# A 32-byte tile at the top of the right-hand SBUF stack, ahead of the pool that holds the parts of X, in a fp32 two-layer transformer kernel

## The chip, the core and the metric

The kernel runs on one core of one Trainium2 chip. The metric is the device time of one launch in microseconds (us); the time given for a kernel is the median of its runs. One more execution was profiled, and all rows of a profile in this document come from profiled executions.

## The reference, cut to what matters

The input is 512 tokens of width 1024 in fp32. Two layers follow each other, each with a gated feed-forward block, a mixer and a second feed-forward block; the last step is a norm.

```
for layer in range(2):
    x = x + 0.5 * swiglu(rmsnorm(x, g[0]), ffn_w_in[layer, 0], ffn_w_out[layer, 0])
    h = rmsnorm(x, g[1])
    x = x + (even_mixer(h, ...) if layer == 0 else odd_mixer(h, ...))
    x = x + 0.5 * swiglu(rmsnorm(x, g[2]), ffn_w_in[layer, 1], ffn_w_out[layer, 1])
return rmsnorm(x, final_norm_g)
```

`swiglu` multiplies by a 1024 x 5632 matrix, gates one half with the silu of the other, and multiplies by a 2816 x 1024 matrix. The even mixer joins gated linear attention with softmax attention that has a forget gate; the odd mixer selects keys with an indexer and attends in a latent space. The output must be as exact as fp32.

## The kernel before, in words

X lies transposed in SBUF: 8 tiles of 128 features by 512 tokens. Every product of two fp32 operands is made of three fp32r products: each operand is split into a high part, which is a rounded copy (ScalarE), and a low part, which is the rest (DVE); high x high, high x low and low x high are summed in PSUM. `mm3` (L207 to L209) issues the three matmuls for one weight block of 128 x 128 and one moving operand of up to 512 columns.

The stages run one after the other: ffn0, even, ffn1, ffn2, odd, ffn3, and the final norm.

*The ffn stages.* The first product of a feed-forward block is done by Winograd's form of Strassen's scheme, seven products p1 to p7 in place of eight, on halves of the tokens (256 columns each) and on halves of the contracted features. `combined` (L231 to L259) makes from X the seven combinations of its quarters (`B11`, `T1`, `B21`, `B22`, `T2`, `T4`, `T3`) and splits them into `th` (high) and `tl` (low): four tiles of each, `[128, 7, 256]` fp32r, which stay for the whole stage. `product` (from L358, the matmul is L366) streams one of the seven slices of 256 columns against 128-column weight blocks: 2 halves of the output x 4 pairs of feature tiles x 3 parts, so 24 matmuls for each of the seven products. The outer loop is over 11 pairs of output tiles; pair 0 of the first stage is done the plain way with 512 columns (96 matmuls of `mm3` on `th`, `tl`). After pairs 3, 7 and 11 the second product of the block runs over what has been gated so far: `down_mm` streams `hh`, `hl` (512 columns) against weights (L207 to L209). The weights come by DMA on SyncE's queue into `wraw`, `a22` and `a12`; DVE combines them (`side`, L132 to L153) and ScalarE and DVE split them (`cut`, L162 and L163) into `whi`, `wlo`, up to three products ahead.

*The mixer stages.* They begin with projections of X. `scaled` (L218) splits X into eight tiles `xgh` and eight `xgl`, `[128, 512]` fp32r. `proj_units` streams them, 512 columns, against weight blocks. `tok_units` (L596 to L608) makes token-major values instead: there slices of 128 columns of `xgh`, `xgl` are the stationary weights, and 256 columns of `whi`, `wlo` are streamed.

*Where the tiles lie.* The tile framework gives out addresses in SBUF (bytes in each partition) from two stacks. The left stack grows up from the bottom; X, `wraw`, `whi`, `wlo`, `hh`, `hl` and the mixers' scratch (`x`, `p`, `pts` and others) lie there. The right stack grows down from the top, and has one pool only, `xp`. `open_in` (L1293) releases and opens it anew for each stage; it holds `th`, `tl`, `te`, `to`, `a22`, `a12` and `ws` in the ffn stages, `xgh` and `xgl` in the mixers, and `fo` at the end. The top of the right stack is byte 229344, which is 32 past a multiple of 64, and every tile of `xp` has a size that is a multiple of 64. So every tile of `xp` begins 32 bytes past a multiple of 64: `th0` at 147424, `tl3` at 197600, `xgh0` at 196576, `xgl0` at 212960. On the left, `X` (16512), `wraw` (47552), `whi` (63936), `wlo` (76224), `hh` (88512), `hl` (108992) and the `x` tiles begin at multiples of 64; `ones`, `ident`, `causal`, `chunkmask` and `cols` (from 33120) begin 32 past one. The pool `xp` reuses the place of scratch tiles of earlier stages, and a tile waits for those whose bytes it takes (`reuse_waits="tile"`).

The order of TensorE's instructions is the program's, written by hand; the other engines' orders are planned by the framework.

```
self.xp = tc.alloc_tile_pool(name="xp", bufs=1, side="right", reuse_waits="tile")
self.TH = [self.xp.tile([128, 7, HT], F32R, name=f"th{j}") for j in range(KT // 2)]
for i, (w, x) in enumerate(((hi, xh), (hi, xl), (lo, xh))):
    mm(o, w[:, c], x, start=fresh and f == j == i == 0, stop=j == 3 and i == 2, skip_group_check=True)
```

Of the kernel before, what the change touches and what calls it, by code (L numbers as in the profile page):

```python
# [8 lines left out]
F32 = mybir.dt.float32  # L9
# [163 lines left out]
class Builder:  # L173
# [1090 lines left out]
    def build(self):  # L1264
        from contextlib import ExitStack
        with ExitStack() as ctx:
            nc, tc = self.nc, self.tc
            pool = lambda name, bufs, **kw: ctx.enter_context(tc.tile_pool(name=name, bufs=bufs, **kw))
# [19 lines left out]
            for t, n in ((self.chunkmask, "chunkmask"), (self.ident, "ident"), (self.causal, "causal"), (self.cols, "cols")):  # L1288
                nc.gpsimd.dma_start(t, self.i[n])

            self.xp = None

            def open_in(kind):  # L1293
# [173 lines left out]
```

## Time and profile before

| what | value |
|---|---|
| median of 3 runs | 1914.0 us |
| the 3 runs | 1907.32, 1914.0, 1915.86 us |
| the profiled execution | 1906.54 us |
| its span, first to last instruction | 1904.7 us |
| mean granted TensorE clock | 0.991 |
| instructions in the profile | 30516 |
| HBM read, written | 178.03 MB, 2.15 MB |

The profiled execution is 1.8 us longer than its span, and is the fastest of those shown. Engines are named PE (TensorE's matmuls), PEld (TensorE's weight loads), DVE, ACT (ScalarE), POOL and SP. A tile's buffer numbers are left out, so `th` stands for th0 to th3. The end of a matmul in the profile is modelled, while its start is recorded; neighbours overlap in the listing.

### The profile page before, as it was taken

The page shows a single profiled execution, that of the slowest core. Times are in us where ns is not written, and L with a number is a line of the kernel's source. Part 1 is how long each engine was busy: PE and PEld are TensorE (multiplying, and loading weights), DVE is VectorE, ACT ScalarE, POOL GpSimd, SP SyncE. Part 2 cuts the span into 40 slices and gives each one's busy share as a digit, 9 for nine tenths or more (in the row PEclk, how much of TensorE's full clock was granted, in tenths as well). Part 3 has the DMA queues.
Part 4 walks back from the last instruction along what each step waited for, and adds up shares of the span by engine and source line. Part 5 has one row for each costly group of instructions (what it writes and reads, how often), then busy time and mean ns, then how long its engine had stood idle before and what let it go on. Part 6 is the DMA issues. An engine that isn't in the chain of part 4 may idle for free.

```text
span 1904.7 us, 30516 instructions
## 1 busy us (share of the span) xinstructions
PE 1858.3 (98%) x12376; PEld 1665.6 (87%) x12376; DVE 1451.5 (76%) x1917; ACT 909.9 (48%) x1286; POOL 218.0 (11%) x211
## 2 busy tenths in 40 slices
PE   8999999999999999999999999999999999999997
PEld 7989899887877999989899998987777789899996
DVE  8979687457557979868897885964898599696774
ACT  6535345334465634525564452543538566353353
POOL 0000000100262000000200000011258320000001
PEclk9999999999999999999999999999999999999998
DMA  5333422223441233322423333234156222423322
GB/s 186 96 107 105 126 86 78 94 80 96 126 122 67 89 110 104 113 97 78 144 89 92 109 100 122 67 107 136 60 162 170 79 94 93 125 89 114 108 67 78
DMA packets 60653, 198.16 MB, mean 104 GB/s; under 512 B 7896, under 2 KB 8072, under 8 KB 57440
## 3 DMA queue, kind: packets, MB, share of 16 engines
q1 hardware_dynamic: 57856, 191.65, 32.2%
q10 hardware_dynamic: 2304, 4.20, 0.8%
q8 instruction: 97, 1.59, 0.3%
q0 software_dynamic: 352, 0.36, 0.1%
q14 instruction: 44, 0.36, 0.1%
HBM read 178.03 MB, written 2.15 MB: 95 GB/s over the span
## 4 chain that ended last, share of the span: by engine, by line
PE 84%; DVE 12%; ACT 2%; issue 1%; DMA 1%; SPq 0%; DVEq 0%; POOL 0%; ACTq 0%; POOLq 0%
PE ps L366 25%; PE pt L366 12%; PE s L209 6%; PE s L208 6%; PE s L207 6%; PE s L366 6%; PE ps L207 3%; PE ps L208 3%; PE ps L209 3%; PE s L730 2%; DVE tl L241 2%; DVE wlo L88 1%; PE o L764 1%; DVE acc L1217 1%; PE pt L749 1%; PE pt L207 1%
## 5 line engine op out<-in xcount | busy, mean ns | idle before, releaser
L366 PE MATMUL ps<-th,wlo 128*128 128x256 f32 x1376 | 384.8, 280 | 2.4 <-DVE wlo L163 2.3
L366 PE MATMUL ps<-th,whi 128*128 128x256 f32 x1376 | 385.2, 280 | 1.3 <-DVE ta L414 1.3
L366 PE MATMUL ps<-tl,whi 128*128 128x256 f32 x1376 | 384.5, 279 | 0.9 <-DVE tl L241 0.9
L84 ACT ACTIVATE whi<-wraw 128x1024 fp32r<-128x1024 f32 (+3 forms) x156 | 157.3, 1010 | 351.0 <-PE s L208 135.5
L366 PEld LDWEIGHTS ps<-th,wlo 128*128 128x128 f32 x1376 | 259.4, 188 | 3.2 <-DVE wlo L163 3.2
L366 PEld LDWEIGHTS ps<-th,whi 128*128 128x128 f32 x1376 | 259.2, 188 | 2.3 <-DVE ta L414 1.5
L366 PEld LDWEIGHTS ps<-tl,whi 128*128 128x128 f32 x1376 | 259.3, 188 | 1.7 <-DVE tl L241 1.1
L209 PE MATMUL s<-hh,wlo 128*128 128x512 f32 x528 | 205.9, 390 | 0.0
L208 PE MATMUL s<-hl,whi 128*128 128x512 f32 x528 | 205.6, 389 | 0.0
L207 PE MATMUL s<-hh,whi 128*128 128x512 f32 x528 | 205.6, 389 | 0.0
L162 ACT ACTIVATE whi<-a 128x1024 fp32r<-128x1024 f32 x131 | 139.0, 1061 | 137.8 <-issue 39.2
L88 DVE TENSOR_TENSOR wlo<-wraw,whi 128x1024 fp32r<-128x1024 f32 (+3 forms) x144 | 169.2, 1176 | 40.3 <-ACT whi L84 39.8
L279 POOL TENSOR_TENSOR ss<-ss,sq 128x512 f32<-128x512 f32 x41 | 65.4, 1596 | 1113.6 <-ACT sq L275 1113.4
L366 PE MATMUL pt<-th,whi 128*128 128x256 f32 x688 | 192.0, 279 | 0.0
L366 PE MATMUL pt<-tl,whi 128*128 128x256 f32 x688 | 191.9, 279 | 0.0
L366 PE MATMUL pt<-th,wlo 128*128 128x256 f32 x688 | 191.9, 279 | 0.0
L163 DVE TENSOR_TENSOR wlo<-a,whi 128x1024 fp32r<-128x1024 f32 x131 | 159.7, 1219 | 6.8 <-ACT whi L162 6.7
L162 ACT ACTIVATE whi<-wraw 128x1024 fp32r<-128x1024 f32 (+1 forms) x89 | 93.6, 1052 | 131.7 <-PE ps L366 51.5
L492 DVE SCALAR_TENSOR_TENSOR dn<-s,R 128x512 f32<-128x512 f32 x72 | 49.7, 690 | 122.3 <-PE s L209 122.3
L162 ACT ACTIVATE whi<-ws 128x1024 fp32r<-128x1024 f32 x86 | 90.7, 1055 | 84.0 <-PE ps L366 51.2
L366 PEld LDWEIGHTS pt<-tl,whi 128*128 128x128 f32 x688 | 129.3, 188 | 0.0
L366 PEld LDWEIGHTS pt<-th,wlo 128*128 128x128 f32 x688 | 129.3, 188 | 0.0
(323 smaller groups left out, 4338.4 us busy)
## 6 DMA issues: line engine op xcount, KB each, us to landing
a<-in_ffn_in_dram SPq DMA_DIRECT2D x88, 512.0 KB, 3.7
wraw<-in_ffn_in_dram SPq DMA_DIRECT2D x87, 512.0 KB, 4.7
wraw<-in_ffn_out_dram SPq DMA_DIRECT2D x64, 512.0 KB, 3.6
wraw<-in_ffn_out_dram SPq DMA_DIRECT2D x32, 384.0 KB, 3.1
x<-x SPq DMA_DIRECT2D x62, 128.0 KB, 2.3
wraw<-in_even_fox_dram SPq DMA_DIRECT2D x4, 1024.0 KB, 4.8
wraw<-in_even_out_dram SPq DMA_DIRECT2D x4, 1024.0 KB, 5.6
wraw<-in_odd_q_dram SPq DMA_DIRECT2D x8, 512.0 KB, 3.2
```

What stands on the lines that cost most here:

```text
L84: nc.scalar.activation(hi, x, AF.Copy)
L88: nc.vector.tensor_sub(lo, x, hi.bitcast(F32))
L162: b.nc.scalar.activation(o[0][:, s], x[:, s], AF.Copy)
L163: b.nc.vector.tensor_sub(o[1][:, s], x[:, s], o[0][:, s].bitcast(F32))
L207: mm(ps, w[0], x[0], start=first, stop=False)
L208: mm(ps, w[0], x[1], start=False, stop=False)
L209: mm(ps, w[1], x[0], start=False, stop=last)
L241: v.tensor_sub(l, src, h.bitcast(F32))
L279: nc.gpsimd.tensor_tensor(self.ss, self.ss, sq, op=OP.add)
L366: mm(o, w[:, c], x, start=fresh and f == j == i == 0, stop=j == 3 and i == 2, skip_group_check=True)
L492: nc.vector.scalar_tensor_tensor(t, bank, 0.5, R, op0=OP.mult, op1=OP.mult)
L730: nc.tensor.matmul(s[:, :n], q[hh][:, b * 128:b * 128 + 128], k[hh][:, :n], start=k is kh, stop=k is kl)
```

## The change

Before the pool `xp` is opened for the first time, one pool of one tile is opened on the same side. The tile has 8 fp32 in each partition, 32 bytes; nothing writes or reads it, and it stays until the end. All tiles of `xp` get addresses that are 32 lower, multiples of 64: `th0` 147392, `xgh0` 196544, and so on.

```diff
             for t, n in ((self.chunkmask, "chunkmask"), (self.ident, "ident"), (self.causal, "causal"), (self.cols, "cols")):
                 nc.gpsimd.dma_start(t, self.i[n])
 
+
+            pool("edge", 1, side="right").tile([128, 8], F32, name="edge")
             self.xp = None
 
             def open_in(kind):
```

## Rows read from the trace of the kernel before

**Rows 1.** Busy time, share of the span and instructions, whole span (page).

```profile
PE 1858.3 (98%) x12376; PEld 1665.6 (87%) x12376; DVE 1451.5 (76%) x1917; ACT 909.9 (48%) x1286; POOL 218.0 (11%) x211
```

**Rows 2.** The chain that ended last, by engine and by line (page).

```profile
PE 84%; DVE 12%; ACT 2%; issue 1%; DMA 1%; SPq 0%; DVEq 0%; POOL 0%; ACTq 0%; POOLq 0%
PE ps L366 25%; PE pt L366 12%; PE s L209 6%; PE s L208 6%; PE s L207 6%; PE s L366 6%; PE ps L207 3%; PE ps L208 3%; PE ps L209 3%; PE s L730 2%; DVE tl L241 2%; DVE wlo L88 1%; PE o L764 1%; DVE acc L1217 1%; PE pt L749 1%; PE pt L207 1%
```

**Rows 3.** PE's groups: names, shapes, count | busy us, mean ns | idle before.

```profile
L366 PE MATMUL ps<-th,whi 128*128 128x256 f32 x1376 | 385.2, 280 | 1.3 <-DVE ta L414 1.3
...
L207 PE MATMUL s<-hh,whi 128*128 128x512 f32 x528 | 205.6, 389 | 0.0
...
L207 PE MATMUL ps<-xgh,whi 128*128 128x512 f32 x208 | 84.2, 405 | 0.0
...
L207 PE MATMUL ps<-whi,xgh 128*128 128x256 f32 x128 | 37.6, 294 | 0.0
```

**Rows 4.** Windows: busy us (instructions) by engine, granted clock, DMA share, GB/s.

```profile
core 0: us, PE busy (x) PEld busy (x) DVE busy (x) ACT busy (x) POOL busy (x), PEclk, DMA share, GB/s
1067.20:1145.60 78.40, 78.40 (x673) 78.37 (x672) 71.05 (x70) 43.19 (x48) 0.00 (x0) 1.00 0.31 100
1145.70:1188.90 43.20, 43.20 (x192) 35.77 (x191) 22.90 (x27) 8.82 (x9) 0.00 (x0) 1.00 0.38 119
1382.80:1421.80 39.00, 39.00 (x169) 31.33 (x168) 38.24 (x93) 12.20 (x16) 19.70 (x13) 1.00 0.63 178
...
614.00:634.00 20.00, 19.00 (x156) 18.40 (x155) 19.83 (x26) 12.07 (x18) 3.86 (x2) 1.00 0.20 61
```

**Rows 5.** Timeline of PE, L366 run, then `hh` run: start, listed us, instruction.

```profile
1067.22 0.28 PE L366 MATMUL ps<-th,whi 128*128 128x256 f32 x1
...
1145.62 0.39 PE L207 MATMUL s<-hh,whi 128*128 128x512 f32 x1
...
1146.78 0.39 PE L209 MATMUL s<-hh,wlo 128*128 128x512 f32 x1
...
1188.94 0.39 PE L209 MATMUL s<-hh,wlo 128*128 128x512 f32 x1
```

**Rows 6.** Timeline of PE, odd mixer, first and last of 168 matmuls.

```profile
1382.70 0.40 PE L207 MATMUL ps<-xgh,whi 128*128 128x512 f32 x1
...
1421.67 0.40 PE L209 MATMUL ps<-xgh,wlo 128*128 128x512 f32 x1
```

**Rows 7.** Timeline of PE, token-major projection, two starts 24 matmuls apart.

```profile
388.09 0.28 PE L207 MATMUL ps<-whi,xgh 128*128 128x256 f32 x1
...
390.93 0.28 PE L207 MATMUL ps<-whi,xgh 128*128 128x256 f32 x1
```

**Rows 8.** Timeline of PE, odd mixer, a pair of score matmuls.

```profile
1328.70 0.40 PE L1227 MATMUL s<-x 128*128 128x256 f32 x2
1328.94 0.40 PE L207 MATMUL ps<-xgh,whi 128*128 128x512 f32 x1
```

**Rows 9.** Timeline of PE's weight loads, two in a row.

```profile
508.87 0.19 PEld L207 LDWEIGHTS ps<-xgh,whi 128*128 128x128 f32 x1
508.98 0.19 PEld L208 LDWEIGHTS ps<-xgl,whi 128*128 128x128 f32 x1
```

**Rows 10.** Groups of ACT, then of DVE, columns as in rows 3.

```profile
L162 ACT ACTIVATE whi<-a 128x1024 fp32r<-128x1024 f32 x131 | 139.0, 1061 | 137.8 <-issue 39.2 <-PE pt L366 39.0 <-PE s L208 29.6
...
L162 ACT ACTIVATE whi<-wraw 128x1024 fp32r<-128x1024 f32 x87 | 92.3, 1061 | 131.2 <-PE ps L366 51.5 <-PE s L366 46.5 <-PE s L208 27.2
L162 ACT ACTIVATE whi<-ws 128x1024 fp32r<-128x1024 f32 x86 | 90.7, 1055 | 84.0 <-PE ps L366 51.2 <-PE s L208 30.0 <-DVE ws L146 2.0
...
L163 DVE TENSOR_TENSOR wlo<-a,whi 128x1024 fp32r<-128x1024 f32 x131 | 159.7, 1219 | 6.8 <-ACT whi L162 6.7
...
L163 DVE TENSOR_TENSOR wlo<-wraw,whi 128x1024 fp32r<-128x1024 f32 x87 | 106.1, 1221 | 14.2 <-ACT whi L162 14.2
```

## The prediction, made before the changed kernel was built or run

> **What bounds the kernel now.** I read the page's busy shares first: PE works 98% of the span, DVE 76% [rows 1]. A high PE share alone says little, because the listed ends of matmuls are modelled, so the second view is the chain that ended last: 84% of it is PE, and 43% is the one line L366 (25, 12 and 6 by bank) [rows 2]. So the pace at which PE starts one matmul after another sets the time. The third view, the groups of PE's lines, cannot give that pace: it lists 280 ns for a 256-column matmul and 389 to 405 ns for a 512-column one [rows 3], and neighbours overlap. The fourth view can. The timeline gives starts, so a pace is the distance between two starts divided by the matmuls between them; the windows show that the stretches used are full and the granted clock is 1.00 there [rows 4].
>
> The paces differ with where the operands lie. In the program as it is, everything in the right-hand pool begins 32 bytes past a multiple of 64, and everything on the left that TensorE reads in these stretches begins at a multiple of 64; slices inside a tile step by 512 bytes or more and keep that.
> - 512 columns streamed from `hh`, `hl` (left), weights left: 42.16 us between starts 5 and 191 of a run, 186 steps, **226.7 ns** [rows 5].
> - 512 columns streamed from `xgh`, `xgl` (right), weights left: 38.97 us for 167 steps, **233.4 ns** [rows 6].
> - 256 columns from `th`, `tl` (right), weights left, L366: 78.40 us for the run's 672 matmuls (7 products of 24 for each of 4 pairs), **116.7 ns** [rows 5]. That is exactly half of 233.4, so this pace goes by streamed columns, with nothing fixed per matmul.
> - 256 columns from the left, weights from the right (token-major projections): 2.84 us for 24 steps, **118.3 ns** [rows 7].
>
> **The change, part by part.** No instruction is added, removed or moved; no queue sees another order. The tile holds no data. All right-hand tiles slide down by 32 bytes together. Their overlap with left tiles of earlier stages could bring or drop a wait, but left tiles begin and end at multiples of 64 in that region, so no right tile crosses an edge by moving from 32 past a multiple to the multiple. Cost of waits: 0.
>
> *(a) L366.* There are 1376 matmuls of each of three kinds into `ps` [rows 3], and by the code 3 x 688 into `pt` and 3 x 344 into `s`: 7224. The case that the trace does not show is a long run of 256 columns with both operands at multiples of 64. Bounds: half of the 512-column pace on the left, 113.35 ns, or the 118.3 ns of rows 7. Two aligned score matmuls of 256 columns (L1227) take 0.24 us, 120 ns each as rounded, near 117 at best [rows 8]; but they stand alone between right-hand matmuls. The first five aligned 512-column matmuls behind L366 are also slow, 1.16 us or 232 ns each, before the run settles at 226.7 [rows 5], so a pair cannot show a settled pace. I take 113.35 because the settled right-hand pace halves exactly from 512 to 256 columns, and because the weight load does not forbid it: where nothing else holds it, two loads start 0.11 us apart [rows 9], less than 113. Gain: 116.67 - 113.35 = 3.32 ns each. Not all count. The first 144 matmuls of three of the four ffn stages run while DVE is 99% busy (19.83 of 20 us) and PE waits for DVE-made parts [rows 4], and some 480 at the first stage's start do too, by the same reason; that leaves about 6300. 6300 x 3.32 = **20.9 us**. In steady stretches DVE is busy 71.05 of 78.40 us [rows 4]; shortened by 672 x 3.32 ns = 2.2 us that is 71.05 / 76.2 = 93%, so DVE still covers. Were that cover gone, DVE's own 71.05 us would be the floor.
>
> *(b) Mixer projections from `xgh`, `xgl`,* 512 columns: 208 of each of three kinds into `ps` [rows 3] and 32 of each into `s`, 720. They go from 233.4 to 226.7, 6.7 ns. The 168 of rows 6 lie where DVE is busy 38.24 of 39 us [rows 4] and gain nothing that lasts. 552 x 6.7 = **3.7 us**. The 96 matmuls of the first pair add 96 x 6.7 = **0.6 us**.
>
> *(c) Token-major projections,* 3 x 128 = 384 [rows 3]: from 118.3 to 113.35, 4.95 ns, **1.9 us**; lower bound 0.
>
> What rows 7 show is that the two reads affect each other: 118.3 ns is slower than the weight load by itself (0.11 us) and than L366's 116.7 with the streamed side misplaced. The Trainium skill, page "SBUF — State Buffer", section "Who interferes with whom", says otherwise: TensorE has two independent read ports and never waits on anyone. By it alignment would be worth nothing and the sum would be 0; the trace disagrees with it by the 6.7 ns between rows 5 and 6.
>
> *(d) The other engines.* ScalarE's copy of 1024 columns takes 1061 ns from right-hand `a`, 1061 from left-hand `wraw`, 1055 from right-hand `ws`; DVE's low part 1219 and 1221 from `a` and `wraw` [rows 10]. Right and left differ by 6 ns at most, on engines that are not the bound: 0, and 86 x 6 ns = 0.5 us either way if it counted. Loads into right-hand tiles keep their size and shape: 0.
>
> Sum: 20.9 + 3.7 + 0.6 + 1.9 = **27.1 us**. The profiled execution took 1906.5 us, so it would take 1879.4; the median shown is 1914.0, 7.5 above it, so I forecast 1914.0 - 27.1 = **1887 us**. What is late next is DVE at the start of each ffn stage, as now.
>
> **The rivals.**
> 1. *Only the 512-column matmuls gain.* With 256 columns the weight load fills nearly the whole step, and the two reads may keep each other at 35/32 of a cycle per column whatever the address, as the 117 ns or so of rows 8 suggest. Then (b) and the first pair alone count: 1914.0 - 4.3 = 1909.7. Against it: rows 8 are unsettled pairs.
> 2. *Half the gain.* The weight load, slowed by the stream beside it, holds the step at 115 ns: 6300 x 1.67 = 10.5, plus 4.3, plus (c) at half, 1.0: 1898. For it: rows 7, where some such slowing exists.
> 3. *The address does not matter,* or the tile does not move the pool. Then 226.7 against 233.4 comes from what runs beside (DVE 53% busy in the one stretch, 98% in the other [rows 4]): 1914. Against it: L366, with DVE at 91%, has the pace of the 98% stretch to the tenth of a ns, which a load on other engines would not give. This is also where the skill's rule named above leads.
> 4. *Slower.* Stream and weights now begin at the same place within 64 bytes and collide in every step without settling, as in the first five of rows 5: 232 / 226.7 = 1.023, so L366 goes to 119.4 ns. 7224 x 2.7 = 19.7 us lost, less 4.3: 1929. It decides against the change above 116.67 + 4.3 us / 7224 = 117.3 ns. Against it: aligned 512-column runs do settle, within five matmuls.
>
> **How the numbers follow.** About 0.5% (9.6 us) is what a measurement of this kernel can tell from no change. Forecast 0.52, rival 1 0.27, rival 2 0.09, rival 3 0.06, rival 4 0.06. Faster by over 0.5%: forecast and rival 2, 0.61. Within: rivals 1 and 3, 0.33. Slower: 0.06. Low end: all 7224 and all 720 gain (24.0 + 4.8 + 0.6 + 1.9 = 31.3 us) from the fastest run shown, 1907.3: 1876; rounded down to 1875. High end: rival 1 from the highest run shown, 1915.9 - 4.3 = 1912. That leaves out rivals 3 and 4 and the odd run.
>
> **What would show it.** Forecast: the L366 run of 672 lasts 76.2 us in place of 78.4, and xgh runs step by 226.7. Rival 1: xgh at 226.7, L366 still 78.4. Rival 2: L366 at 77.3. Rival 3: xgh still 233.4. Rival 4: L366 over 79. I am wrong in the sum, not the mechanism, if L366 shows 113.35 but PE's waits for DVE grow by more than a few us.

## The result and the profile after

| what | before | after |
|---|---|---|
| median of 4 runs | 1912.96 us | 1935.3 us |
| lowest, highest | 1907.32, 1915.86 us | 1927.92, 1939.01 us |
| the profiled execution, its span | 1906.54, 1904.7 us | 1939.01, 1937.2 us |
| mean granted clock in it | 0.991 | 0.986 |
| instructions | 30516 | 30516 |

The ratio is **1.0116 [1.0077, 1.0154]**: slower by 1.2%, 22.3 us by the medians. The forecast was 1887 us. The profiled execution of after is the longest of its four, so spans overstate the difference; settled paces don't, and the ledger below goes by them.

First the page of after: busy time, then the chain that ended last by engine and by line.

```profile
PE 1886.5 (97%) x12376; PEld 1695.8 (88%) x12376; DVE 1456.0 (75%) x1917; ACT 910.2 (47%) x1286; POOL 216.6 (11%) x211
...
PE 84%; DVE 11%; ACT 2%; issue 1%; DMA 1%; SPq 0%; POOL 0%; DVEq 0%; ACTq 0%; POOLq 0%
PE ps L366 25%; PE pt L366 12%; PE s L207 6%; PE s L208 6%; PE s L209 6%; PE s L366 6%; PE ps L207 3%; PE ps L208 3%; PE ps L209 3%; PE s L730 2%; DVE tl L241 1%; PE o L764 1%; DVE wlo L88 1%; DVE acc L1217 1%; PE pt L749 1%
```

Beside [rows 1, 2], the chain has the same shape, and ACT's busy time is the same within 0.3 us and DVE's within 4.5. PE and PEld are longer by 28.2 and 30.2 us for the same 12376 instructions. So PE does the same work at another pace. The groups of PE's lines say where, as far as listed durations can:

```profile
L366 PE MATMUL ps<-th,whi 128*128 128x256 f32 x1376 | 390.0, 283 | 1.2 <-DVE ta L414 1.2
...
L207 PE MATMUL s<-hh,whi 128*128 128x512 f32 x528 | 205.6, 389 | 0.0
...
L207 PE MATMUL ps<-xgh,whi 128*128 128x512 f32 x208 | 83.8, 403 | 0.9 <-DVE x L1138 0.8
...
L207 PE MATMUL ps<-whi,xgh 128*128 128x256 f32 x128 | 38.3, 299 | 0.0
```

Against [rows 3], the lines with 256 streamed columns went up (280 to 283, 294 to 299 ns), `hh` stood still, and `xgh` went down by 2 ns. The size has to come from starts. The timeline of PE in after, the same places as [rows 5 to 7], in order of time:

```profile
387.38 0.28 PE L207 MATMUL ps<-whi,xgh 128*128 128x256 f32 x1
...
390.26 0.28 PE L207 MATMUL ps<-whi,xgh 128*128 128x256 f32 x1
...
1085.25 0.28 PE L366 MATMUL ps<-th,whi 128*128 128x256 f32 x1
...
1165.88 0.40 PE L207 MATMUL s<-hh,whi 128*128 128x512 f32 x1
...
1404.12 0.39 PE L207 MATMUL ps<-xgh,whi 128*128 128x512 f32 x1
...
1409.79 0.39 PE L208 MATMUL ps<-xgl,whi 128*128 128x512 f32 x1
...
1443.77 0.39 PE L209 MATMUL ps<-xgh,wlo 128*128 128x512 f32 x1
```

- The L366 run of 672: 1165.88 - 1085.25 = 80.63 us, **120.0 ns** a step, where [rows 5] have 78.40 us and 116.7 ns.
- Token-major projections: 2.88 us for 24 steps, **120.0 ns**, where [rows 7] have 118.3.
- 512 columns from `xgh`: the first 25 steps take 5.67 us, **226.8 ns**, where [rows 6] have 233.4. The whole run of 168 takes 39.65 us for 167 steps, 237.4 each, so it became longer all the same.

Windows of after show what bounds each stretch (busy us and instructions of PE, PEld, DVE, ACT, POOL; then granted clock, DMA share, GB/s):

```profile
358.70:624.60 265.90, 259.86 (x1517) 213.44 (x1516) 159.77 (x275) 119.94 (x225) 56.63 (x79) 0.96 0.31 96
...
1085.20:1165.80 80.60, 80.60 (x673) 80.56 (x673) 71.16 (x70) 43.16 (x48) 0.00 (x0) 1.00 0.30 98
1166.00:1209.20 43.20, 43.20 (x192) 35.75 (x191) 22.77 (x27) 8.71 (x9) 0.00 (x0) 1.00 0.38 121
...
1404.20:1443.90 39.70, 38.76 (x169) 31.08 (x168) 38.94 (x91) 12.19 (x16) 18.62 (x12) 1.00 0.57 165
```

In the L366 window PE is full and DVE's work is what it was (71.16 against 71.05 us [rows 4]): no new wait, only longer steps. In the `xgh` window DVE is busy 38.94 of 39.70 us, and the group of `xgh` above has 0.8 us of waiting for DVE's `x` that [rows 3] don't have: PE's shorter steps wait for DVE there. The `hh` window is as before to the tenth.

**The ledger.** Four runs of 672 went from 78.40 to 80.63 us, four of 504 from 58.80 to 60.47, three of 504 from 58.89 to 60.55 and the run of 384 in the first stage from 46.49 to 47.65: 8.9 + 6.7 + 5.0 + 1.2 = 21.8 us, nearly all of the 22.3 us between the medians. The rest of the 32.5 us between the two profiled executions is mostly the mixers (even 261.2 to 266.0, odd 256.6 to 260.8), and the granted clock in the even window is 0.96; the same window of before, 353.6 to 614.7, has 0.99. After has stretches at the lower of the two clock levels at 480.7 (13.7 us) and 1446.6 (10.2 us), before at 480.4 (3.4 us) and 1425.8 (6.8 us). The other runs of after are 3 to 11 us shorter than the profiled one.

### The profile page after: what moved, and what is told of

It is laid out like the page before. It is cut to its first block, busy times and chain, and to the rows that moved or that the text cites. A ratio compares the mean times of both kernels' runs of the same rounds, so it can differ in the third digit from the quotient of the medians.

```text
span 1937.2 us, 30516 instructions
## 1 busy us (share of the span) xinstructions
PE 1886.5 (97%) x12376; PEld 1695.8 (88%) x12376; DVE 1456.0 (75%) x1917; ACT 910.2 (47%) x1286; POOL 216.6 (11%) x211
## 4 chain that ended last, share of the span: by engine, by line
PE 84%; DVE 11%; ACT 2%; issue 1%; DMA 1%; SPq 0%; POOL 0%; DVEq 0%; ACTq 0%; POOLq 0%
PE ps L366 25%; PE pt L366 12%; PE s L207 6%; PE s L208 6%; PE s L209 6%; PE s L366 6%; PE ps L207 3%; PE ps L208 3%; PE ps L209 3%; PE s L730 2%; DVE tl L241 1%; PE o L764 1%; DVE wlo L88 1%; DVE acc L1217 1%; PE pt L749 1%
## 5 line engine op out<-in xcount | busy, mean ns | idle before, releaser
L366 PE MATMUL ps<-th,wlo 128*128 128x256 f32 x1376 | 389.7, 283 | 2.3 <-DVE wlo L163 2.3
L366 PE MATMUL ps<-th,whi 128*128 128x256 f32 x1376 | 390.0, 283 | 1.2 <-DVE ta L414 1.2
L366 PE MATMUL ps<-tl,whi 128*128 128x256 f32 x1376 | 389.4, 283 | 0.0
L366 PEld LDWEIGHTS ps<-th,wlo 128*128 128x128 f32 x1376 | 264.0, 192 | 2.9 <-DVE wlo L163 2.9
L366 PEld LDWEIGHTS ps<-th,whi 128*128 128x128 f32 x1376 | 264.0, 192 | 2.1 <-DVE ta L414 1.4
L366 PEld LDWEIGHTS ps<-tl,whi 128*128 128x128 f32 x1376 | 264.1, 192 | 0.6
L366 PE MATMUL pt<-th,whi 128*128 128x256 f32 x688 | 194.9, 283 | 0.0
L366 PE MATMUL pt<-th,wlo 128*128 128x256 f32 x688 | 194.7, 283 | 0.0
L366 PE MATMUL pt<-tl,whi 128*128 128x256 f32 x688 | 194.7, 283 | 0.0
L366 PEld LDWEIGHTS pt<-tl,whi 128*128 128x128 f32 x688 | 132.1, 192 | 0.0
L366 PEld LDWEIGHTS pt<-th,whi 128*128 128x128 f32 x688 | 132.1, 192 | 0.0
L366 PEld LDWEIGHTS pt<-th,wlo 128*128 128x128 f32 x688 | 132.1, 192 | 0.0
```

## The experiments

All distances below count bytes from the place of the stationary operand (the weights `whi`, `wlo`) to that of the streamed one, modulo 256. Before, `th` stands 32 past; after, 0.

**One half of the change at a time** (12 runs of the first kernel, 6 of the second). The tile of 32 bytes goes into the stage's own pool, behind `xgl`, or behind `tl`:

```diff
# e1_xg_only
                     self.XGL = [self.xp.tile([128, S], F32R, name=f"xgl{i}") for i in range(KT)]
+                    self.xp.tile([128, 8], F32, name="edge")
# e2_th_only
                     self.TL = [self.xp.tile([128, 7, HT], F32R, name=f"tl{j}") for j in range(KT // 2)]
+                    self.xp.tile([128, 8], F32, name="edge")
```

The stack grows down and each stage opens it anew, so in the first only the mixers' X parts move to multiples of 64, in the second only the ffn stages'.

> Only xgh and xgl (the mixers' parts of X) lie at multiples of 64; th, tl and the rest of the right-hand pool stay 32 past one, as in the kernel before. Theory (the loss is in L366 alone: a 256-column matmul costs 120.0 ns with both operands at multiples of 64 and 116.7 ns with the streamed one 32 past): L366 stays at 116.7 ns, 512-column matmuls on xgh, xgl go from 233.4 to 226.7 ns, and 720 of them less the 168 beside a busy DVE give 552 x 6.7 ns = 3.7 us: about 0.2% faster than before, ratio 0.998. Rival (the mixers lose too, as the two profiled executions show with 4.9 and 4.2 us more in them): ratio 1.004 or so, about 9 us slower.

> Only th and tl lie at multiples of 64; all other right-hand tiles (te, to, a22, a12, ws, xgh, xgl) stay 32 past one. Theory (L366 alone): 7224 x 3.33 ns = 24.1 us slower at most, 21 to 24 us in all, ratio 1.011 to 1.013, L366 at 120.0 ns in its runs. Rival (part of the loss comes from the tiles that ScalarE, DVE and the DMA queues write and read, a22, a12, ws, te, to): clearly less than 21 us, and the busy time of DVE and ScalarE as before.

Measured: `e1_xg_only` 1911.8 us, ratio 1.0009 [0.9993, 1.0024], no difference; `e2_th_only` 1932.2, ratio **1.0116 [1.0098, 1.0133]**, the whole loss. The timeline of PE in `e2_th_only` has the L366 run at 80.63 us:

```profile
1086.07 0.28 PE L366 MATMUL ps<-th,whi 128*128 128x256 f32 x1
...
1166.70 0.40 PE L207 MATMUL s<-hh,whi 128*128 128x512 f32 x1
```

In `e1_xg_only` L366 keeps 116.7 ns, `xgh` streams go at 226.7 and token-major ones at 120.0, as in after. The mixers do not gain from it. By comparing the start of the same matmul in both traces, the even mixer was 1.05 us ahead by 534 us, and a stretch of 3.4 us at the lower clock level at 547.6 took it back; the odd one loses up to 3 us where DVE is the bound. Such stretches come and go without a change of the mixers: `e2_th_only`, whose mixers lie as in before, has 13.7 us at the lower level at 480.6 and an even mixer of 267.3 us, longer than that of after. In the odd mixer of `e1_xg_only` the window over the 168 steps reads as that of after:

```profile
1388.50:1428.20 39.70, 38.76 (x169) 31.08 (x168) 38.94 (x91) 12.19 (x16) 18.61 (x12) 1.00 0.57 166
```

One DVE instruction in that window became longer. Timelines of DVE and POOL, first before (its DVE row merges the instruction with the next one of `L1220`):

```profile
1394.98 0.55 DVE L1220 TENSOR_SCALAR acc<-acc 128x256 f32<-128x256 f32 x2
1395.05 2.94 POOL L86 TENSOR_TENSOR wlo<-wraw,whi 128x1024 fp32r<-128x1024 f32 x1 [1.93 <-ACT whi L84]
```

and after:

```profile
1416.16 2.39 POOL L86 TENSOR_TENSOR wlo<-wraw,whi 128x1024 fp32r<-128x1024 f32 x1 [1.77 <-ACT whi L84]
1416.24 2.46 DVE L1220 TENSOR_SCALAR acc<-acc 128x256 f32<-128x256 f32 x1
```

By itself the DVE instruction takes 279 ns in before and 2460 in after. It takes some 2460 in all four traces with the mixers at distance 0 (after, `e1_xg_only` and, of the kernels below, `e3_weights_moved` and `e4_half_load_aligned`), where POOL's `L86` begins 76 to 85 ns ahead of it; in the other ten it takes 276 to 280, and `L86` takes 2.90 to 3.07 us in place of 2.39. So in each trace one of the two is long, and it is DVE's where POOL starts clearly first. That is 2.2 us more on the engine that bounds the stretch, beside the 2.6 us by which the odd mixer of `e1_xg_only` is longer than that of before; that the one causes the other was not tested.

**Alignment or distance** (one run). In after, both operands are at multiples of 64, so either their own alignment or their distance could be what costs. Two tiles of 32 bytes around the weights' pool move the weights alone: `th` and the weights are then both 32 past a multiple of 64, at distance 0. `hh` goes up by 64 bytes, keeps its place at a multiple of 64, and is 32 from the weights.

```diff
+            pool("edge0", 1).tile([128, 8], F32, name="edge0")
             self.wsp = pool("wsp", 3)
+            pool("edge1", 1).tile([128, 8], F32, name="edge1")
```

> The right-hand pool stays 32 past a multiple of 64, and the split weights whi and wlo are moved by 32 too, so that L366 has both operands 32 past. Theory (what counts is where the streamed operand lies against the weight that is being loaded): L366 goes to 120.0 ns, xgh and xgl streams to 226.7 ns, and the hh, hl streams, now 32 apart from their weights, to 233.4 ns. Rival (each operand's own place against a multiple of 64 counts): L366 near 121 to 122 ns, as the two misplacements add up (3.3 ns for the stream, about 1.6 ns for the weights), xgh and xgl stay at 233.4 or slower.

Measured: 1941.6 us beside 1909.3. The timeline of PE, L366 run, then the `hh` run:

```profile
1084.34 0.28 PE L366 MATMUL ps<-th,whi 128*128 128x256 f32 x1
...
1164.98 0.40 PE L207 MATMUL s<-hh,whi 128*128 128x512 f32 x1
...
1209.55 0.39 PE L209 MATMUL s<-hh,wlo 128*128 128x512 f32 x1
```

80.64 us for 672 steps is 120.0 ns again with neither operand at a multiple of 64, and `hh`, still at one, goes from 226.7 to 44.57 / 191 = 233.4 ns a step; `xgh`, now at distance 0, goes at 226.7 to 227. **What counts is the distance between the two, not where either lies.** `hh` and `xgh` swap paces when the weights move.

**All distances** (four kernels, one run each). Tiles of other sizes at the same two places give each ffn stage and each mixer a distance of its own:

```diff
                     self.TL = [self.xp.tile([128, 7, HT], F32R, name=f"tl{j}") for j in range(KT // 2)]
+                    n = (64, 96, 128, 160)[self.nth]
+                    self.nth += 1
+                    self.xp.tile([128, n // 4], F32, name="edge")
```

> th and tl of the four ffn stages lie at four other places: 64, 96, 128 and 160 bytes below where the kernel before has them, so at 32, 64, 96 and 128 bytes below the weights' place, counted in multiples of 512 (before: 32 above it; in the changed kernel: at it). xgh and xgl of the two mixers lie 64 and 96 bytes lower. Theory (the streamed operand and the weight being loaded get in each other's way, and their distance decides; it repeats every 64 bytes): ffn0 and ffn2 (an odd number of 32s) at 116.7 ns a step, ffn1 and ffn3 (whole 64s) at 120.0. Rival (the distance counts over a longer period, as the 118.3 ns of the token-major projections, 32 the other way, suggests): ffn0 at 118.3 ns and at least one other pace among the rest.

> The same with 192, 224, 256 and 288 bytes for the four ffn stages (160, 192, 224 and 256 below the weights' place), and 128 and 160 for the mixers. Theory (repeats every 64 bytes): ffn0 and ffn2 at 116.7 ns, ffn1 and ffn3 at 120.0. Rival (a longer period): other paces than these two; a distance with a pace below 116.7 ns would make a kernel faster than both, 7224 matmuls times the difference.

> The four ffn stages with th, tl 320, 352, 384 and 416 bytes lower (288, 320, 352 and 384 below the weights' place), the mixers with 192 and 256. From the paces so far (0: 120.0 ns, 32 above: 116.7, 32 below: 118.3, 64 below: 117.8 and in one run 113.3, 96 below: 118.7, 128 and 160 below: 120.0, 192 below: 117.8, 224 below: 116.7, 256 below: 120.0). Theory (distance over a period of 512 bytes, with a settled pace for each): four more settled paces between 113.3 and 120.0 ns. Rival (a period of 256 bytes): 288 below as 32 below, 118.3; 320 as 64 below, 117.8 or 113.3; 352 as 96 below, 118.7; 384 as 128 below, 120.0 ns.

> 448 and 480 bytes lower in ffn0 and ffn1 (416 and 448 below the weights' place), and 96 lower (64 below) again in ffn2 and ffn3, where one run of 504 matmuls had shown 113.3 ns and two others 117.8. Theory (more than one settled pace for this distance, chosen by how a run begins): ffn2 and ffn3 show 117.8 and 113.3 again, in the same runs as in ffn1 before, since the starts are the same. Rival (the 113.3 ns of that run had another cause, such as what ran beside): 117.8 ns in all of them.

Measured: 1919.0, 1927.5, 1916.5 and 1912.1 us, each the mixture of its stages' paces. The settled paces, all at the granted clock of 1.00, from starts over runs of 504 or 672 (256 columns) and shorter stretches (512 columns):

| distance, bytes | 256 columns, ns | 512 columns, ns |
|---|---|---|
| 0 | 120.0 | 226.7 |
| 32 | 116.7 | 233.3 |
| 64 | 117.8 | 228.9 or 233.2 |
| 96 | 120.0 | 233.3 |
| 128 | 120.0 or 118.7 | 232 to 233.4 |
| 160 | 118.7 | 234.3 |
| 192 | 117.8 or **113.3** | 233.3 |
| 224 | 118.3 | 233.3 |

A stage whose X parts lie 256 bytes lower has the same pace: `s2_places` repeats 116.7 with 256 bytes in its third stage and 120.0 with 288 in its fourth. The paces of `s3_places`, 288 to 384 bytes below the weights, are those of 32 to 128 below. So the table goes round every 256 bytes, not every 64 and not only every 512. At 192 bytes there are two settled paces. Timeline of PE in `s1_places`, second stage, its first run (504) and its second (672):

```profile
639.35 0.60 PE L328 MATMUL s<-ident,Rc 128*128 128x128 f32 x4
639.71 0.37 PE L366 MATMUL ps<-th,whi 128*128 128x256 f32 x1
...
696.92 0.39 PE L207 MATMUL s<-hh,whi 128*128 128x512 f32 x1
...
729.35 0.39 PE L209 MATMUL s<-hh,wlo 128*128 128x512 f32 x1
729.58 0.28 PE L366 MATMUL ps<-th,whi 128*128 128x256 f32 x1
...
808.73 0.39 PE L207 MATMUL s<-hh,whi 128*128 128x512 f32 x1
```

The run behind the four transposes takes 57.21 us for 504 steps, 113.5 ns with its first slow step; the run behind the `hh` stream takes 79.15 us for 672 steps, 117.8. Same addresses, same instructions: only what stood ahead differs, and each pace holds to the end of its run. It came out so in the three other ffn stages placed at 192 too, one in `s3_places` and two in `s4_places`, as the expectation of `s4_places` has it. 192 is not the only such distance. At 128 the runs of 504 behind the four transposes go at 118.7 and those behind `hh` at 120.0; at 64 a run of 48 matmuls of 512 columns goes at 233.2 where the others go at 228.9; and token-major streams, too short to stand in the table, go at 117.8 and then 116.7 at distance 32 and at 117.3 or 118.5 at distance 160. At distances 0, 32 and 64 all runs of 504 and 672 with full loads went at one pace, whatever stood ahead.

**What the load costs** (one run each). If a step were the stream plus a share of its weight load, half the load should shorten it. Ten of the twelve matmuls of each sum in L366, and nearly all of the second product, load and use 64 of the 128 weight columns; half of the output rows are left out of these sums. One kernel does it on after (distance 0), one on before (distance 32).

```diff
-                        mm(o, w[:, c], x, start=fresh and f == j == i == 0, stop=j == 3 and i == 2, skip_group_check=True)
+                        if (j, i) in ((0, 0), (3, 2)):
+                            mm(o, w[:, c], x, start=fresh and f == j == i == 0, stop=j == 3 and i == 2, skip_group_check=True)
+                        else:
+                            mm(o[:64], w[:, c][:, :64], x, start=False, stop=False, skip_group_check=True)
```

> The changed kernel (all at multiples of 64), in which 10 of the 12 matmuls of each sum in L366, and nearly all of the second product on hh, hl, load and use only 64 of the 128 weight columns; so half of the output rows are left out of these sums. Theory (each weight load costs the stream a fixed 32 cycles, 13.3 ns, one for every 4 weight columns): matmuls behind a half load lose 16 cycles, L366 has steps of 113.3 ns there where nothing else waits, hh streams 220 ns. Rival (the stream's own columns cost, whatever the load: 32 in 256 and 32 in 512): L366 stays at 120.0 and hh at 226.7 ns. If DVE becomes the bound in the ffn stages, only steps without a wait count.

> The kernel before (th, tl 32 above the weights' place) with the same sums cut to 64 of the 128 weight columns as in the run with half loads at multiples of 64; half of the output rows are left out of these sums. There, L366's steps had gone from 120.0 to 113.3 ns behind half loads where the pace had settled. Theory (the weight loads cause the stream's loss at this distance too): the 24 lost cycles of 256 columns go to about 12, steps of 111.7 ns, at most 113.3. Rival (at this distance the loss belongs to the stream, 3 cycles in 32 columns whatever is loaded): 116.7 ns as before.

Measured: 1908.1 us beside 1909.3 of before, and 1928.0 beside 1907.7. Timeline of PE, a run of 672 and the `hh` stream behind it, `e4_half_load_aligned`:

```profile
1068.47 0.28 PE L367 MATMUL ps<-th,whi 128*128 128x256 f32 x1
...
1145.75 0.39 PE L494 MATMUL s<-hh,whi 128*128 128x512 f32 x1
```

and `e5_half_load_offset`:

```profile
1080.03 0.28 PE L367 MATMUL ps<-th,whi 128*128 128x256 f32 x1
...
1159.55 0.40 PE L494 MATMUL s<-hh,whi 128*128 128x512 f32 x1
```

The runs of 672 take 77.28 us at distance 0, 115.0 ns where full loads take 120.0, and 79.52 us at distance 32, 118.3 ns where full loads take 116.7. Timelines of PE around the two full loads between two sums, distance 0:

```profile
1110.90 0.28 PE L369 MATMUL ps<-th,whi 128*64 128x256 f32 x1
1111.02 0.28 PE L369 MATMUL ps<-tl,whi 128*64 128x256 f32 x1
1111.13 0.28 PE L367 MATMUL ps<-th,wlo 128*128 128x256 f32 x1
1111.25 0.28 PE L367 MATMUL ps<-th,whi 128*128 128x256 f32 x1
1111.37 0.28 PE L369 MATMUL ps<-tl,whi 128*64 128x256 f32 x1
```

and distance 32:

```profile
1111.26 0.28 PE L367 MATMUL ps<-th,whi 128*128 128x256 f32 x1
1111.38 0.28 PE L369 MATMUL ps<-tl,whi 128*64 128x256 f32 x1
...
1112.10 0.28 PE L369 MATMUL ps<-tl,whi 128*64 128x256 f32 x1
```

In this run at distance 0 the step from one full load to the other takes 120 ns and the next one 117; of the steps between two half loads, two thirds take 113 or 114 and the rest 116 or 117. At distance 32, the six half-load steps shown take 0.72 us, 120 ns each, and those of the whole run 118.2 on average. The `hh` steps at distance 0 went to 229.7 ns on average, slower than the 226.7 of full loads, in both kernels. So a shorter load helps the 256-column stream at one distance and harms it at the other, and no expectation held whole in either run; the nearest is one run of 504 in `e5_half_load_offset`, which takes 116.9 ns a step where the six others take 118.3 to 118.5. The edit halves the output rows that a matmul writes along with the load, and these runs don't part the two. The load (or these rows) is part of the cost at distance 0, but not as a fixed price that each one adds; mixing two sizes of load may also keep a stream from settling. The mechanism inside TensorE stays open.

**A version from the table** (5, 12 and 6 runs). Distance 192 has the fastest pace of all, if the run starts well. A tile of 96 bytes puts `th`, `tl` there in all ffn stages, and transposes of the identity into the bank that the next product overwrites stand ahead of the two runs of each stage that follow an `hh` stream: four in `v1_kick4`, one in `v2_kick1`. `v3_kick4_mixers` is `v1_kick4` with tiles of 224 bytes in the mixers, for 113.3 in the token-major projections.

```diff
                     d = st[p] = {"a": self.bank("ps")}
+                    if p in (GROUPS[1][0] + 1, GROUPS[2][0] + 1):
+                        for t in range(4):
+                            nc.tensor.transpose(d["a"][:, :128], self.ident, self.ident)
                     product(p, q, d["a"], B11, True)
```

> A version after what the runs before showed: th and tl 96 bytes lower than before in all four ffn stages (64 below the weights' place), where a run of L366 settled at 113.3 ns when it began behind four transposes and at 117.8 ns when it began behind the 512-column stream of hh; so four transposes of the identity are put ahead of the runs of 672 and 504 matmuls, into the bank that the first product starts anew. Theory (the pace that a run settles at is chosen by how stream and weight loads stand to each other where it begins): the runs of 672 last 76.2 us plus 0.45 for the transposes in place of 78.4, those of 504 57.1 plus 0.45 in place of 58.8, and with the run of 504 at the start of each stage (57.1, without any addition) the whole is 17 to 19 us faster than before, ratio 0.990 to 0.991. Rival (the transposes do not choose): 117.8 ns in those runs, 4 stages x (1176 x 1.1 ns + 0.9) less 4 x 1.9 us: about the time of before, ratio 1.000 to 1.002.

> The same with one transpose in place of four. Theory (any instruction whose weight load is longer than its stream is enough to let the load fall behind): as with four, and 0.34 us less for each of 8 runs, ratio 0.989. Rival (it needs several): 117.8 ns in the runs behind it, ratio 1.000.

> The version with four transposes, and the mixers' xgh, xgl 224 bytes lower than before, where the token-major projections had settled at 113.3 ns and the 512-column streams at 228.9 ns. Theory: 384 x 5 ns and 720 x 4.5 ns, 5.1 us if all of it counted, less what lies beside a busy DVE: 2 to 5 us faster than with four transposes alone. Rival (as with xgh and xgl at multiples of 64, the mixers give nothing back, since other work sets their length): the same time as with four transposes alone, within 0.2%.

Measured, beside 1909.1 us of before:

| kernel | median, us | ratio to before |
|---|---|---|
| `v1_kick4` | 1892.8 | 0.9910 [0.9895, 0.9926] |
| `v2_kick1` | 1909.5 | 0.9997 [0.9983, 1.0012] |
| `v3_kick4_mixers` | 1887.8 | 0.9892 [0.9871, 0.9913] |

Timeline of PE in `v1_kick4`, a run of 672 behind its four transposes:

```profile
1062.65 0.60 PE L443 MATMUL ps<-ident 128*128 128x128 f32 x4
1063.00 0.37 PE L366 MATMUL ps<-th,whi 128*128 128x256 f32 x1
...
1139.26 0.39 PE L207 MATMUL s<-hh,whi 128*128 128x512 f32 x1
```

and in `v2_kick1`, a run of 504 behind one:

```profile
1186.04 0.27 PE L443 MATMUL ps<-ident 128*128 128x128 f32 x1
1186.06 0.36 PE L366 MATMUL ps<-th,whi 128*128 128x256 f32 x1
...
1245.50 0.39 PE L207 MATMUL s<-hh,whi 128*128 128x512 f32 x1
```

76.26 / 672 = 113.5 ns, first slow steps included, and 59.44 / 504 = 117.9. All four runs of 672 and all seven of 504 in `v1_kick4` are at 113.5. Its gain adds up: 4 x (78.40 - 76.26) + 4 x (58.80 - 57.22) + 3 x (58.89 - 57.22) + 1.2 for the run of 384 = 21.1 us, less eight groups of transposes at 0.35 us, 2.8: 18.3; 16.3 was measured. The profiled executions differ by 13.2 us, and there the rest can be read: the even mixer of `v1_kick4` takes 265.2 us in place of 261.2, with 13.7 us at the lower clock level from 471.3, the first stage's start is 1.8 us longer, and the odd mixer 0.8 us shorter. `v3_kick4_mixers` is faster than before and after; its median is 4.9 us under that of `v1_kick4`, as expected, but the two intervals overlap, so a gain from the mixers is not shown. Its windows of a run of 672 and one of 504 answer the question of DVE's cover:

```profile
1057.10:1133.30 76.20, 76.20 (x675) 76.20 (x674) 70.47 (x70) 42.33 (x48) 0.00 (x0) 1.00 0.33 102
1177.30:1234.40 57.10, 57.10 (x507) 57.10 (x505) 52.23 (x52) 31.54 (x36) 0.00 (x0) 1.00 0.21 66
```

DVE is busy 70.47 / 76.20 = 92% and PE has no gap.

## Why the prediction was wrong

**Reading of the bound: right.** PE's steps set the time, listed durations do not show them and starts do. Nearly all that was lost came out of L366's steps (21.8 of 22.3 us), and the groups of L366 in after have 0.0 to 2.5 us of idle time ahead of them, as in before (0.0 to 2.8).

**The rule drawn from rows 5 to 7: wrong, and the root of the rest.** The prediction saw that paces differ with where the operands lie, and read it as alignment: right-hand tiles misplaced, left-hand ones well placed. Each of its streams differed in distance as well, and `e3_weights_moved` parted the two: distance decides. The three rows were samples of a table of eight distances (0 for `hh`, 32 for `xgh` and `th`, 224 for the token-major streams), and the table has no single good place: 0 is the best for 512 columns and, with 96, the worst for 256.

**(a) L366: the failed step.** The forecast took 113.35 ns because the pace at distance 32 halves exactly from 512 to 256 columns, "with nothing fixed per matmul", and carried that halving to distance 0. Measured: 120.0, so the halving holds at 32 only. At distance 0 a 512-column step of 226.7 ns is 544 cycles of the 2.4 GHz level, 32 over its columns, and a 256-column step of 120.0 is 288, 32 over as well. At distance 32 the steps are 560 and 280, 48 and 24 over. One halving in one place does not show how another place scales. The upper bound, 118.3 from [rows 7], was also too low. No settled row of before had the case: the pair of [rows 8] reads as 120 ns each only because the starts are rounded (in the trace they are 1328.703, 1328.820 and 1328.937, 117 ns a step), the same pair takes 117 and 118 ns in after, not the settled 120.0, so the prediction set it aside with reason. What it lacked was a settled row at this distance with this column count, and it put a halving in its place. In place of 6300 x 3.32 = 20.9 us gained, the runs lost 21.8.

**The weight load: dismissed for a wrong reason.** That a load alone needs 0.11 us [rows 9] does not say what it needs beside a stream. `e4_half_load_aligned` took 5.0 ns off the step by halving most loads at distance 0 (and the output rows with them), so that the load has a part in the step there is likely, if not shown apart from these rows. `e5_half_load_offset` added 1.6 ns by the same edit at distance 32, so no fixed price fits.

**The rule of the Trainium skill.** With nothing changed but addresses, L366's step differs by 3.3 ns between before and `e2_th_only`. The Trainium skill, page "SBUF — State Buffer", section "Who interferes with whom", gives TensorE two independent read ports that wait for no one. Read as a statement on time, these runs do not bear it out. The prediction was right to set it aside (rival 3 is out), but it had no other rule that told the sign.

**(b) Mixer projections: pace right, gain not there.** 233.4 went to 226.7 as forecast. `e1_xg_only` shows no time for it: where DVE is the bound the steps wait (the prediction had left out the 168 for that), DVE itself has 2.2 us more there in the one instruction beside POOL's, and the microsecond gained elsewhere is smaller than what stretches of the lower clock give and take.

**(c) Token-major projections: wrong sign.** 118.3 became 120.0, not 113.35, a loss of 384 x 1.7 ns = 0.7 us in place of 1.9 gained. The stated lower bound of 0 had no reason against a loss behind it.

**(d) Other engines, waits, DVE's cover: right in the ffn stages.** ACT's and DVE's copies keep their times within 5 ns (the largest change is DVE's from `wraw`, 1221 to 1226), no wait was added ahead of L366, and `v3_kick4_mixers` has DVE at 92% where 93% was forecast for a run of 76.2 us. In the odd mixer "0" was not right: there stand the 2.2 us of `L1220`.

**The rivals.** Rival 4 came nearest: with stream and weights at the same place every step of L366 is slower, and its run lasts "over 79". Its price, 119.4 ns, is 0.6 under the measured one, and its time, 1929, is 6.3 us under the median: L366 too low by 7224 x 0.6 = 4.3 us, and the 4.3 us of (b) and the first pair that it subtracted did not come, 8.6 against 6.3. It had 0.06 because `hh` settles within five steps at distance 0; it settles, but a stream of 256 columns settles at a slow pace. Rival 1's doubt ("with 256 columns the weight load fills nearly the whole step") named a place worth looking at, as `e4_half_load_aligned` suggests, and held the pace at 116.7 where it rose.

## What to carry to other kernels

Where every matmul brings its own weights of 128 columns, as here, the pace depends on the distance between the streamed and the stationary operand in SBUF modulo 256 bytes, and the best distance for 512 columns is one of the two worst for 256: measure the settled step from starts over some hundred matmuls for each column count, and place tiles by that table, not by alignment. A pace read at one distance must not be scaled to another, and where no row shows the case at hand, a range that spans the neighbouring cases can still miss it. Where a step has two settled paces, what runs just ahead chooses: four cheap transposes were worth 0.9% here, one was worth nothing.

## What the runs showed of the hardware that was not expected

- Settled steps of 256 columns with a load of 128 columns each run from 113.3 to 120.0 ns by distance and, at some distances, by what stood ahead, at the same granted clock; the table repeats every 256 bytes.
- At distance 192 two paces, 113.3 and 117.8 ns, each hold for a whole run of 504 or 672, chosen by what stands ahead of it. At distance 0 the runs of 504 behind the same four transposes stay at 120.0, so a start does not help everywhere.
- Loads of half the columns make a stream of 256 faster at distance 0 (115.0 for 120.0) and slower at distance 32 (118.3 for 116.7). Why was not found, nor why the distance matters at all; no run here looks inside the step.
- DVE's `L1220` takes 279 ns or 2460 ns: the long time stands in the four traces where POOL's `L86` begins 76 to 85 ns ahead of it, and in the ten others `L86` is the longer one, 2.90 to 3.07 us for 2.39.
